# A row-wise infinity norm: implied waits dropped, a zeroing moved to GpSimd, a tail of 32 loads in place of 34

## Chip, cores, metric

One core of one Trainium2 chip. The metric is device time in microseconds (us) of one execution. The kernel before took 627.4 us (median of 3 runs, 627.34 to 628.16). A profile's span, from its first instruction to its last, is some 2.7 us shorter than the time; both are quoted as such.

## The reference

```python
rows, cols = 8192, 8192            # x is float32, 268.4 MB
np.linalg.norm(x, ord=np.inf, axis=1)   # per row: the largest absolute value
```

Every byte of x must be read once; the result is 32 KB.

## The kernel before

All loads are issued by SyncE (SP) into three buffers of 64 KB per partition, and VectorE (DVE) reduces them. 24 whole loads of 8.39 MB, the bulk, are reduced by one instruction each. The last 64 MiB, the tail, come in smaller and smaller loads, so that VectorE catches up with the stream: after the last byte only a small reduction should be left.

```python
TAIL = [
    [9728, 6656],
    [5632, 10752],
    [9600, 6784],
    [9344, 7040],
    [6784, 6528, 3072],
    [4736, 3072, 4224, 4352],
    [3968, 2432, 3072, 2944, 1792, 2176],
]
LAST = (
    [(0, w) for w in (2176, 2048, 1664, 1664)]
    + [(1, w) for w in (1536, 1280, 1152, 1024, 896, 896, 768)]
    + [(0, 640), (1, 640)]
)
...
    part = outp.tile([P, n_tail - B, k_max], F32)
    nc.vector.memset(part[:], 0.0)
...
    for a in range(A):                       # the bulk, 24 times in all
        for n in range(G):
            t = sbuf.tile([P, W + PAD], F32, tag="t")
            nc.sync.dma_start(out=t[:, :W], in_=x_b[a, n])
            absmax(r_bulk[:, a, n * B : (n + 1) * B], ...)
    for i, loads in enumerate(TAIL):         # partial maxima into part
        ...
            absmax(part[:, i * B + b, k : k + 1], t[:, lo : lo + n])
    for j, (b, w) in enumerate(LAST):        # the last buffer
        ...
        if j == len(LAST) - 4:               # store of the bulk maxima
            ins = nc.scalar.dma_start(out=out_b, in_=r_bulk[:])
            after(ins, done, mybir.DependencyClass.Sync)
    nc.sync.dma_start(out=out_t, in_=r_tail[:])
```

A load into a buffer that was used before waits for two things: that VectorE has read the buffer, and that the earlier load into it has landed. The second is implied by the first, since VectorE itself waited for that load. An instruction with two waits is issued as a separate EVENT_SEMAPHORE for one and the instruction itself with the other.

## Time and profile before

| | before |
|---|---|
| time, median of 3 | 627.4 us |
| span of the profile | 624.7 us |
| load queue, share of 16 DMA engines' time | 99.6% |
| VectorE busy | 89% |
| bulk: time between two landings (41 to 467 us) | 19.337 us, 433.8 GB/s |
| tail: last engine's landing of the 24th load to that of the last load | 156.27 us |
| SyncE's separate semaphore waits in the stream | 30, 17 ns each (one 28 ns) |

Two views carry the reading: the DMA row with its queue shares, which says that the stream never pauses, and the chain of waits in time order, where each "issue" of 0.02 us marks the landing that a reduction waited for. The prediction below shows these lines. In them DVE is VectorE, POOL is GpSimd, ACT is ScalarE, and SPq or DVEq is the sequencer that issues SyncE's or VectorE's instructions; q1 is the DMA queue of the loads, q10 that of the store of the bulk maxima and q14 that of the instruction fetches, each with its packets, MB and share of the 16 DMA engines' time. A load's landing is the moment at which its completion is reported.

### The profile page before, as it was taken

How to read it: one execution, taken by the hardware profiler on the slowest of the kernel's cores; microseconds unless marked ns; L12 is line 12 of the kernel's file. 1: busy time of each engine (PE TensorE's matmuls, PEld its weight loads, DVE VectorE, ACT ScalarE, POOL GpSimd, SP SyncE). 2: the span in 40 equal slices, each digit the busy share in tenths (PEclk: the TensorE clock that was granted, in tenths of full speed). 3: DMA queues.
4: the chain of work that ended last, by engine and by line, in shares of the span. 5: the costliest groups of instructions: out<-in, count | busy, mean ns of one | idle time of the engine just before them, and what ended most of it. 6: DMA issues, size and time to landing. Idle time of an engine off the chain costs nothing.

```text
span 624.7 us, 189 instructions
## 1 busy us (share of the span) xinstructions
DVE 553.0 (89%) x67; POOL 0.2 (0%) x4
## 2 busy tenths in 40 slices
DVE  0588988889988889888898888988889999999999
POOL 0000000000000000000000000000000000000000
DMA  9999999999999999999999999999999999999998
GB/s 403 462 411 453 420 449 424 432 441 403 470 403 470 403 470 403 453 420 453 420 441 432 424 449 403 470 403 470 403 438 425 445 417 443 421 427 432 423 423 342
DMA packets 9138, 268.48 MB, mean 430 GB/s; under 512 B 1712, under 2 KB 1712, under 8 KB 3248
## 3 DMA queue, kind: packets, MB, share of 16 engines
q1 hardware_dynamic: 8352, 268.44, 99.6%
q10 hardware_dynamic: 784, 0.02, 0.1%
q14 instruction: 2, 0.02, 0.0%
HBM read 268.44 MB, written 0.03 MB: 430 GB/s over the span
## 4 chain that ended last, share of the span: by engine, by line
DMA 67%; DVE 31%; issue 1%; another core or an unknown queue 0%; DVEq 0%; SPq 0%
DMA t<-in_x_dram 67%; DVE r_bulk L180 24%; DVE part L180 6%; DVE t L180 2%; DVEq L270 0%; DVE r_tail L180 0%; SPq L199 0%
## 5 line engine op out<-in xcount | busy, mean ns | idle before, releaser
L180 DVE TENSOR_REDUCE r_bulk<-t 128x2 f32<-128x16384 f32 x24 | 413.3, 17220 | 69.7 <-DMA t<-in_x_dram 69.7
L180 DVE TENSOR_REDUCE part<-t 128x1 f32<-128x8192 f32 (+20 forms) x28 | 121.5, 4411 | 0.3 <-DMA t<-in_x_dram 0.3
L180 DVE TENSOR_REDUCE t<-t 128x1 f32<-128x1664 f32 (+8 forms) x11 | 16.7, 1577 | 0.1
L180 DVE TENSOR_REDUCE r_tail<-t 128x1 f32<-128x644 f32 (+1 forms) x2 | 1.6, 818 | 0.0
L177 DVE MEMSET part<- 128x56 f32 x1 | 0.1, 105 | 0.9 <-PEq L259 0.9
L180 DVE TENSOR_REDUCE r_tail<-part 128x14 f32<-128x56 f32 x1 | 0.2, 202 | 0.0
L259 POOL MEMSET const-bfloat16-1.0<- 128x1 bf16 x1 | 0.1, 103 | 0.0
L259 POOL MEMSET const-uint8-127<- 128x1 uint8 x1 | 0.1, 102 | 0.0
L259 POOL MEMSET const-float32-0.0<- 128x1 f32 x1 | 0.1, 100 | 0.2 <-issue 0.2
L259 POOL MEMSET const-float32-1.0<- 128x1 f32 x1 | 0.1, 99 | 0.0
## 6 DMA issues: line engine op xcount, KB each, us to landing
t<-in_x_dram SPq DMA_DIRECT2D x2, 3392.0 KB, 37.2
t<-in_x_dram SPq DMA_DIRECT2D x1, 5376.0 KB, 40.5
t<-in_x_dram SPq DMA_DIRECT2D x1, 4864.0 KB, 32.9
t<-in_x_dram SPq DMA_DIRECT2D x1, 4800.0 KB, 32.8
t<-in_x_dram SPq DMA_DIRECT2D x1, 4672.0 KB, 34.7
t<-in_x_dram SPq DMA_DIRECT2D x3, 1536.0 KB, 36.9
t<-in_x_dram SPq DMA_DIRECT2D x1, 3520.0 KB, 42.7
t<-in_x_dram SPq DMA_DIRECT2D x1, 3328.0 KB, 40.4
```

The lines of the kernel that those rows point to most:

```text
L177: nc.vector.memset(part[:], 0.0)
L180: return nc.vector.reduce_max(out=o, in_=i, axis=X, apply_absolute_value=True)
L259: nc = _bacc.Bacc("TRN2", target_bir_lowering=False, num_devices=1)
```

## The change

Its intent: fewer instructions on SyncE and VectorE between a landing or a release and what follows it, no work for VectorE in the opening, and less overhead per transfer in the tail.

```diff
-    [9728, 6656],
-    [5632, 10752],
-    [9600, 6784],
+    [4736, 11648],
+    [12928, 3456],
+    [7040, 9344],
     [9344, 7040],
-    [6784, 6528, 3072],
-    [4736, 3072, 4224, 4352],
-    [3968, 2432, 3072, 2944, 1792, 2176],
+    [3584, 6784, 6016],
+    [5376, 4864, 1792, 4352],
+    [4096, 3584, 3200, 2944, 2560],
 ]
 LAST = (
-    [(0, w) for w in (2176, 2048, 1664, 1664)]
-    + [(1, w) for w in (1536, 1280, 1152, 1024, 896, 896, 768)]
-    + [(0, 640), (1, 640)]
+    [(0, w) for w in (2176, 1792, 1792, 1664)]
+    + [(1, w) for w in (1664, 1408, 1280, 1152, 1024, 896)]
+    + [(0, 768), (1, 768)]
 )
+def drop_implied_waits(nc):
+    ...                       # upto[n]: what VectorE had waited for by its n-th count
+            if i.engine == sp and own and len(waits) > 1:
+                known = upto[own - 1]
+                insts[n] = rewait(i, [s for s in waits
+                    if s.id == counter or s.wait_value > known.get(s.id, 0)])
+        elif i.engine == dve and own and len(waits) > 1:
+            ...               # a load that itself waited for VectorE's count implies it
+                insts[n] = rewait(i, [s for s in waits if s.id != counter])
+def clear_partials_early(nc):
+    ...                       # moves the memset ahead of GpSimd's drain, before the barrier
-    nc.vector.memset(part[:], 0.0)
+    nc.gpsimd.memset(part[:], 0.0)
+    nc.at_finalize(clear_partials_early)
+    nc.at_finalize(drop_implied_waits)
```

## The prediction

> **What bounds the kernel now.** I read the page first, for the busy shares and the DMA row; then the queue's share; then the chain of waits in order of time, for the two ends; then the waits of SyncE's queue and the views of single lines, for the waits that the change removes.
>
> ```profile
> span 624.7 us, 189 instructions
> DVE 553.0 (89%) x67; POOL 0.2 (0%) x4
> DMA  9999999999999999999999999999999999999998
> DMA packets 9138, 268.48 MB, mean 430 GB/s; under 512 B 1712, under 2 KB 1712, under 8 KB 3248
> q1 hardware_dynamic: 8352, 268.44, 99.6%
> q14 instruction: 2, 0.02, 0.0%
> ```
>
> VectorE is busy 89% of the span, the load queue 99.6% of sixteen engines' time, and no slice of the DMA row falls below 9 before the last. So the transfer of 268 MB is the bound, from the first packet to the last. A change that adds and removes no bytes can win only at the opening, after the last byte, or in what each transfer costs beyond its bytes. The next lines are from the chain of waits of the same kernel (start, length, what); an "issue" of 0.02 us ahead of a reduction is the landing of the load that it waited for.
>
> ```profile
> 41.24 0.02 issue
> ...
> 466.66 0.02 issue
> ...
> 612.24 0.02 issue
> 612.26 9.90 DVE t L180 x8
> 622.16 0.23 issue
> 622.39 0.59 DVE r_tail L180
> 622.98 0.08 issue
> 623.06 0.88 DVEq L270
> ```
>
> The second of the 24 whole loads landed at 41.24 us and the last at 466.66 us: 425.42 / 22 = 19.337 us for each 8.39 MB, 433.8 GB/s. The remaining 64 MiB is the tail, in 34 loads. Its last landing is the last of the four VectorE semaphore waits in this view of line L180, which ran at about 622.96 us:
>
> ```profile
> L180 DVEq EVENT_SEMAPHORE  x4: 21/21/21, 478.2 to 623.0; - x4
> L180 DVE TENSOR_REDUCE r_tail<-t x2: 817/818/820, 622.4 to 623.1; 128x1 f32<-128x644 f32 x1, 128x1 f32<-128x647 f32 x1
> ```
>
> So the tail took about 622.95 - 466.66 = 156.29 us where eight whole loads would take 8 x 19.337 = 154.70 us: 1.59 us more for 26 more loads, about 0.06 us each. Behind the last landing lie 0.17 us until the last reduction starts (623.12), its 0.82 us, and the output's transfer.
>
> **What the Trainium skill says.** "DMA: Bandwidth & Descriptors", section Specifications, gives the fabric ceiling into SBUF as 435 GB/s; the bulk loads at 433.8 GB/s sit at it, so the transfer rate has no room. (The same table's HBM limit per core, about 358 GB/s, does not agree: this trace reads faster.) "Perfetto Trace Analysis", section Sequencer-only Instruction, says that the profiler shows such an instruction's execution, not its wait; so the 17 ns of an EVENT_SEMAPHORE on SyncE is what is left of an extra wait once its semaphore is there. "VectorE: DVE Perf Modes", section on the TRN2 errata, gives VectorE reading SBUF a fixed cost of 58 cycles and one cycle an element at 0.96 GHz. Here the 768-element reduction starts at 621.53 and the next at 622.39: 0.86 us = 0.80 for the elements + 0.06, which agrees. "Runtime: NRT & Kernel Launch", section Instruction fetch mechanics, says that a sequencer fetches its further instructions by its own DMA queue, mostly hidden. The trace has such a queue with two packets (q14 above), each of 8 KB; by the packet records they ran at 592.0 and 609.4 us, in the midst of the tail.
>
> **The change part by part.**
>
> *Waits of SyncE.* The instruction order shows that all 21 later bulk loads lose the wait on the lane's previous landing and keep the one on VectorE, as do most first loads of the tail's buffers and the last store. Removed is mostly the separate EVENT_SEMAPHORE:
>
> ```profile
> L187 SPq EVENT_SEMAPHORE  x21: 17/17/17, 22.0 to 408.7; - x21
> DMA to landing us min/median/max: 22.0/40.7/59.4
> ```
>
> With lines 199, 224 and 242 there are 21 + 7 + 1 + 1 = 30 of them, of which I expect one to remain: 29 x 17 ns = 0.5 us of SyncE. None is on the path: they run as soon as the landing comes (the first at 22.0 us), and then SyncE waits up to 17.2 us for VectorE, which is the wait that stays:
>
> ```profile
> SPq L187 <- DVE r_bulk L180: 361.6, 21, 17.2
> SPq L187 <- DMA t<-in_x_dram: 54.8, 21, 20.1
> ```
>
> And a bulk load lands a median 40.7 us after its issue, twice its own 19.3 us, so it stands behind a whole load in the queue. Issuing it some 20 ns earlier moves no byte. Worth 0.
>
> *Waits of VectorE.* Two of its four separate waits go: on the first partial maximum and on the first load of the last buffer, each a few tens of ns, 123 and 17 us before the end. VectorE has caught up with the loads again by then or is behind for other reasons. The two waits ahead of the final reductions stay. Worth 0.
>
> *The memset.* 0.105 us leaves VectorE at 0.87 us, where VectorE waits until 22 us for data: 0. On GpSimd a memset of 42 elements comes ahead of the opening barrier. Its four others start 0.03 us apart, so this is 0.03 to 0.1 us, and SyncE's drain ends after GpSimd's anyway (0.43 + 0.126 = 0.56 against 0.30 + 0.18 = 0.48). Should it delay the barrier, it delays the second load's issue from 0.79 us, while the first load, issued at 0, keeps the queue busy to 22 us: 0.
>
> *The tail.* Two loads fewer, the same 64 MiB: 2 x 0.06 = 0.12 us earlier. The last two loads grow from 640 to 768 columns, so the last reduction grows from 647 to 774 elements, 127 x 1.04 = +0.13 us behind the last landing. I also ran the widths through an estimate built from the figures above (a landing every 0.06 us + 19.28 us per 16384 columns, a reduction start every 1.04 ns per element + 0.06 us): VectorE is no more than 0.03 us late at the last load of either list, and the ends differ by 0.01 us. The tail's recutting is thus a wash: -0.12 + 0.13.
>
> *Two side effects.* First, the instruction fetches. The 609.4 us one, by the landing records, set one DMA engine back some 0.9 us, which made it the last of the sixteen for all later loads by about 0.27 us. SyncE loses 31 of its 93 recorded instructions; if one of the fetches is SyncE's, it falls away or comes after the end. Whether that is the harmful one I cannot tell: at even odds, -0.13 us. Second, the store of the bulk maxima is released after the fourth load from the end. There are then 896 + 768 + 768 = 2432 columns to come instead of 768 + 640 + 640 = 2048, 0.45 us more of loading, so its 784 small packets may fall among the last loads where before they just missed them. They took 6 us together, 0.38 us on each engine; with turns taken packet by packet I put it at +0.05 to +0.3, say +0.1 us.
>
> Sum: 0 + 0 + 0 + (-0.12 + 0.13) - 0.13 + 0.1 = about -0.02 us. Leaning a little to the removed fetch, -0.1: 627.4 - 0.1 = 627.3 us.
>
> **The rivals.** (1) The dropped waits were binding and the loads now start early enough to matter: against it stands the DMA row of 9s and the queue's 99.6%. All idle engine time before the last landing, 0.4% or 2.5 us with both ends in it, would be the most to gain: 625 us. (2) VectorE becomes the bound of the tail, since it has larger pieces at the end and no spare wait: its busy row is 9 from slice 31 on, and 1.04 ns an element against 1.18 ns for a load leaves it 12% per element, less 0.06 us a piece. If it fell behind at the end by a piece, that would add up to 0.9 us: 628.3 us. (3) The store collides with the last loads in full and the fetch still hits: +0.4 us, 627.8 us. (4) The harmful fetch is gone and the store slips through: -0.3 us, 627.1 us.
>
> **Range and chances.** All mechanisms together span 626.8 to 628.0 us around 627.3. The three runs of before span 627.34 to 628.16, a scatter as large as any of these terms, upward. I take 626.6 to 628.1. Two per cent is 12.5 us, five times all the idle DMA time, so faster by that is all but excluded; slower needs a stall in the load queue that no part of the change brings, or a hidden cost in a run's state. Chances: 0.005, 0.985, 0.01.
>
> **What would show it right or wrong.** In the profile after: mean GB/s still 430 and the load queue at 99.6%; about 30 SyncE semaphore waits fewer with the median time from issue to landing of the bulk loads unchanged at 40.7 us (if it grew or the bulk loads landed closer than 19.34 us, rival 1 lives); VectorE's 69.7 us of waiting for bulk data unchanged; the last bulk landing at 466.6 us to within 0.1; the last landing near 622.8; the final reductions at about 0.95 us; the store's issue near 621.1. Fewer packets on the instruction queue would support the first side effect, an unchanged two with the same lag at the end would refute it. I would be wrong if the bulk landings move, or the end goes by more than 0.7 us with no step above to carry it.

## The result

| | before | changed |
|---|---|---|
| time, median of 6 runs | 627.62 us (627.34 to 628.16) | 627.43 us (627.33 to 628.26) |
| span of the profile | 624.7 us | 624.7 us |
| instructions in the profile | 189 | 154 |

The ratio is 0.9998, with a 95% interval from 0.9985 to 1.0011: the same. A ratio is the mean time of one kernel's fast runs over that of the other's of the same rounds, so not quite the ratio of the medians.

The page of the changed kernel, the same rows as in the prediction:

```profile
span 624.7 us, 154 instructions
DVE 552.6 (88%) x64; POOL 0.3 (0%) x5
DMA  9999999999999999999999999999999999999998
DMA packets 8849, 268.47 MB, mean 430 GB/s; under 512 B 1680, under 2 KB 1680, under 8 KB 3216
q1 hardware_dynamic: 8064, 268.44, 99.6%
q14 instruction: 1, 0.01, 0.0%
```

35 instructions are gone and the stream is the same: 99.6%, 430 GB/s, no slice below 9 before the last. The instruction queue has one packet in place of two. The changed kernel's chain of waits in time order (start, length, what):

```profile
41.29 0.02 issue
...
447.29 0.02 issue
...
621.92 0.20 issue
622.12 0.80 DVE r_tail L262
622.93 0.06 issue
622.99 0.94 DVE r_tail L262
```

The 2nd load lands at 41.29 us and the 23rd at 447.29: 406.00 / 21 = 19.333 us a load, against 19.337. The last reduction starts at 622.99 us, 0.13 us sooner than before (623.12), and takes longer, as the view of line L262 shows beside VectorE's separate waits, now two and not four:

```profile
L262 DVEq EVENT_SEMAPHORE  x2: 21/21/21, 621.9 to 622.9; - x2
L262 DVE TENSOR_REDUCE r_tail<-t x2: 943/944/945, 622.1 to 623.0; 128x1 f32<-128x772 f32 x1, 128x1 f32<-128x774 f32 x1
```

So it ends at 622.99 + 0.945 = 623.93 us, where before it ended at 623.12 + 0.820 = 623.94. And the waits of SyncE's queue (who for whom: us in total, times, longest):

```profile
SPq L269 <- DVE r_bulk L262: 417.2, 21, 37.5
```

Before, 361.6 us of this stood under VectorE and 54.8 us under the landings: 416.4 us, and now 417.2 us. SyncE waits as long as before, and now in one wait instead of two. The separate waits were gone, the waiting was not. Nor do the bulk's loads land sooner after their issue than before (22.0/40.7/59.4), as the view of the line that issues them shows:

```profile
DMA to landing us min/median/max: 22.0/40.7/59.5
```

The other signs named in the prediction came too: the 24th landing at 466.65 us, the last at 622.88, the store's issue at 621.24. VectorE's waiting for bulk data is 70.6 us and not 69.7, since without the memset its first wait counts from the start (22.0 us in place of 21.0).

### The profile page after: what moved, and what is told of

It is laid out like the page before. It is cut to its first block, busy times and chain, and to the rows that moved or that the text cites. A ratio compares the mean times of both kernels' runs of the same rounds, so it can differ in the third digit from the quotient of the medians.

```text
span 624.7 us, 154 instructions
## 1 busy us (share of the span) xinstructions
DVE 552.6 (88%) x64; POOL 0.3 (0%) x5
## 3 DMA queue, kind: packets, MB, share of 16 engines
q1 hardware_dynamic: 8064, 268.44, 99.6%
## 4 chain that ended last, share of the span: by engine, by line
DMA 64%; DVE 36%; issue 0%
DMA t<-in_x_dram 64%; DVE r_bulk L262 22%; DVE part L262 11%; DVE t L262 3%; DVE r_tail L262 0%
## 5 line engine op out<-in xcount | busy, mean ns | idle before, releaser
L262 DVE TENSOR_REDUCE r_bulk<-t 128x2 f32<-128x16384 f32 x24 | 413.3, 17220 | 70.6 <-DMA t<-in_x_dram 70.6
L262 DVE TENSOR_REDUCE part<-t 128x1 f32<-128x8192 f32 (+18 forms) x27 | 121.5, 4569 | 0.7 <-DMA t<-in_x_dram 0.7
L262 DVE TENSOR_REDUCE t<-t 128x1 f32<-128x1792 f32 (+7 forms) x10 | 16.2, 1687 | 0.0
L262 DVE TENSOR_REDUCE r_tail<-t 128x1 f32<-128x772 f32 (+1 forms) x2 | 1.8, 944 | 0.0
L262 DVE TENSOR_REDUCE r_tail<-part 128x14 f32<-128x42 f32 x1 | 0.2, 186 | 0.0
```

The lines of the kernel that those rows point to most:

```text
L262: return nc.vector.reduce_max(out=o, in_=i, axis=X, apply_absolute_value=True)
```

## The experiments

To compare parts of a tenth of a microsecond, the runs' times are too coarse, so I also read the landing records of each trace: every load has 16 landings, one from each DMA engine. "Tail" below is the mean of the 16 landings of the last load less the mean of the 24th load's; "lag" is how far the last engine's landing of the last load stands behind that mean; "end" is the time from that last landing to the end of the last reduction. A "fetch" is a packet on the instruction queue after the start.

| kernel | loads in tail | fetches, of which in tail | 24th landing, us | tail, us | lag, us | end, us |
|---|---|---|---|---|---|---|
| before | 34 | 2, 2 | 466.66 | 156.074 | 0.67 | 1.009 |
| before, repeated | 34 | 2, 2 | 466.71 | 156.067 | 0.45 | 1.019 |
| memset alone | 34 | 2, 2 | 466.86 | 156.067 | 0.75 | 1.017 |
| waits alone | 34 | 1, 1 | 467.00 | 156.035 | 1.19 | 0.965 |
| tail alone | 32 | 2, 2 | 467.30 | 155.974 | 0.71 | 1.072 |
| changed | 32 | 1, 1 | 466.65 | 155.928 | 0.78 | 1.053 |
| changed, repeated | 32 | 1, 1 | 466.82 | 155.926 | 0.81 | 1.053 |
| changed, 30 more VectorE instructions | 32 | 1, 0 | 467.12 | 155.876 | 0.80 | 1.051 |
| changed, store one load later | 32 | 1, 1 | 467.44 | 155.929 | 0.71 | 1.084 |

The tail's mean repeats to 0.01 us for the same number of loads and fetches; the 24th landing does not, and differs by 0.8 us over these rows without regard to the kernel.

### The waits alone

```diff
  # the kernel before, with the function as in the changed kernel
+    nc.at_finalize(drop_implied_waits)
```

> The kernel before with the implied waits dropped and nothing else. Main theory (the load stream is the bound and the dropped waits were already met when SyncE or VectorE came to them): time within 0.1% of before, bulk landings 19.34 us apart, SyncE's separate semaphore waits down from 30 to about 1. Of the two instruction fetches the one at 609 us is SyncE's, so this kernel shows one packet on the instruction queue and not two, the last engine no longer lags, and the last landing comes 0.2 to 0.3 us before 622.93 us. Rival (the waits were on the path): some 29 x 17 ns to 29 x 50 ns are won, 0.5 to 1.5 us, and the bulk landings move closer. Rival for the fetch (both fetches are VectorE's or neither depends on SyncE's count): two packets stay and the last landing stays at 622.9 us.

627.53 us against 627.42 us of before in the same rounds, ratio 1.0001 (0.9987 to 1.0015). The instruction queue's row of its page:

```profile
q14 instruction: 1, 0.01, 0.0%
```

And the waits of its SyncE queue, the row of the bulk's loads:

```profile
SPq L243 <- DVE r_bulk L236: 417.6, 21, 37.3
```

One separate wait is left on SyncE's loads, as foretold (the view of its loads' lines shows one EVENT_SEMAPHORE), and one fetch; SyncE waits 417.6 us for VectorE in the bulk and for nothing else there. The rival of waits on the path falls. The times alone could not exclude 0.5 us, but in the trace the bulk landings are 19.355 us apart and so not closer than the 19.337 before, and the tail is 0.04 us shorter. My forecast of the last landing was wrong, though: it came at 623.55 us, later than before's 622.93. By the means of 16 landings, +0.14 of these 0.62 us are the bulk (24th load), -0.04 the tail and +0.52 the lag, which rose from 0.67 to 1.19 us: the one fetch left hit an engine that stood 0.28 us behind the mean already and made it the last, at +1.21 us. So a removed fetch takes its time from the mean (156.035 against 156.07), but the last landing depends on which engine the other one hits.

### The memset alone

```diff
  # the kernel before
-    nc.vector.memset(part[:], 0.0)
+    nc.gpsimd.memset(part[:], 0.0)
+    nc.at_finalize(clear_partials_early)
```

> The kernel before with only the zeroing moved to GpSimd ahead of the barrier. Main theory: nothing but the opening changes; second load issued within 0.05 us of 0.79 us, first landing at 22.0 us, two instruction fetches, last landing at 622.9 us, span 624.7 us. Rival (the memset delays the barrier and with it the stream): second issue later by 0.1 us or more and every landing after the first later by as much.

One run, 627.66 us, beside a median of 627.42 us (627.32 to 627.71) for before on the same chip. The opening in the timeline (start, length, engine, line, operation):

```profile
0.00 1.14 SPq L223 DMA_DIRECT2D t<-in_x_dram  x2
0.37 0.14 POOL L213 MEMSET part<- 128x56 f32 x1
```

The memset takes 0.14 us at 0.37 us. The records have the second load's issue at 0.81 us, 0.02 us later than the 0.79 before, and the first landing at 21.99 us (21.96). Tail, fetches and end are those of before. The last landing and the span missed their forecasts by 0.3 us (623.22 and 625.0 us); 0.22 us of it stands in the mean of the 24th landing already, 0.07 us in the lag. The second landing is 0.04 us later than before's, not the 0.1 us or more of the rival. The part is worth nothing either way.

### The tail alone

```diff
  # the kernel before, with the changed TAIL and LAST
```

> The kernel before with only the new tail of 32 loads, all waits kept. Main theory: two loads fewer bring the last landing forward by 0.12 us, the later start of the last reduction's 0.945 instead of 0.820 us takes it back, time within 0.1% of before; two instruction fetches, the SyncE one again late in the tail. The store of the bulk maxima meets the last load and costs it about 0.05 us. Rival (the tail is where the change wins or loses, and another part cancels it): the span moves by more than 0.3 us either way.

627.58 us against 627.42, ratio 1.0004 (0.9991 to 1.0016). Its queue row keeps both fetches:

```profile
q14 instruction: 2, 0.02, 0.0%
```

The table gives the two terms cleanly. Two loads fewer are worth 156.07 - 155.974 = 0.10 us, 0.05 us each. The larger last piece costs 1.072 - 1.01 = 0.06 us. Both have the foretold sign; the second is half as large as I had it. The rival's sign came by its letter, for the profiled span is 625.4 us, 0.7 us more than before's. But 0.64 us of that is there at the 24th landing (467.30 us), before the new tail has an effect, and the last landing at 623.55 us is late for the same reason. So the rival, large parts that cancel, falls by the tail and the end in the table.

### Thirty more instructions on VectorE

```diff
  # the changed kernel; pad is a new [P, 1] tile, and clear_partials_early
  # is made to look at GpSimd's memsets alone
+    for _ in range(30):
+        nc.vector.memset(pad[:], 0.0)     # one column, in VectorE's idle opening
```

> The changed kernel with 30 one-column memsets on VectorE in the opening, in the 21 us in which it waits for the first load. Main theory (the remaining fetch is VectorE's, comes after a fixed number of its instructions, and sets one DMA engine back by the fetch plus about one packet of the load under way): the fetch moves from 587 us to about 290 to 320 us, into whole loads with packets of 2.42 us; one engine falls behind by 2.4 to 2.8 us for good; the last landing moves from 622.88 to about 624.8 us and the time to about 629.4 us (+0.3%). Rival 1 (the fetch is not VectorE's): it stays at 587 us and the time stays at 627.4 us. Rival 2 (it is VectorE's, but the cost does not depend on the packets): it moves and costs 0.9 us as before, time 627.4 us.

627.85 us against 627.42, ratio 1.0007 (0.9994 to 1.0019). The queues in the stretch from 290 to 300 us:

```profile
q1 hardware_dynamic: 81, 4.26, 98.7%
q14 instruction: 1, 0.01, 0.2%
```

The fetch moved from 586.95 us to 296.56 us. In both kernels 47 of VectorE's recorded instructions had started by then, while SyncE stood at 50 and at 19. So this fetch is VectorE's and comes at about the same count of its instructions (45 to 50 of the recorded ones over these traces). The other went with 29 of SyncE's instructions and two of VectorE's. It was no second one of VectorE's: before, it came 10 recorded VectorE instructions after the first, and here 53 more started after the fetch without another. It is then SyncE's by elimination.

The second half of my theory is refuted, rival 2 is right. The fetch ran 0.309 us, and the load packet behind it took 3.044 us instead of 2.418: 0.309 + 0.626 = 0.94 us for one engine. In the tail, with packets of 0.25 to 0.65 us, the same sum is 0.72 us and 0.92 us (before, the second with two slow packets behind the fetch), 0.98 us (changed) and 0.99 us (waits alone). A fetch sets one engine back by 0.7 to 1.0 us, whatever the packets. Over 16 engines that is about 0.05 us of the mean, which the table has: 155.928 with the fetch in the tail, 155.876 without.

### One buffer: the disputed waits on the path

```diff
  # the kernel before; for the second run also drop_implied_waits
-    BUFS: int = 3,
+    BUFS: int = 1,
```

> The kernel before with one load buffer instead of three, all waits kept: now every load waits for VectorE on the path that sets the time, so that a dropped wait has its best chance to show in the next run. A whole load should take 17.2 us of reduction + about 1 us until the first packet + 19.3 us, some 37.7 us instead of 19.34; in all about 1100 us.

> The same with one buffer and the implied waits dropped. Main theory (an implied wait is by its nature met before the wait that stays, so its 17 ns are over while SyncE still waits for VectorE): the bulk landings come as far apart as in the run with the waits kept, to within 0.02 us, and the time agrees within 0.1%. Rival (a dropped wait saves its own time even so, 17 to 60 ns in each of some 30 loads): 0.5 to 2 us less, landings 0.02 to 0.06 us closer.

1178.44 us with the waits kept, 1178.18 us with them dropped, ratios 1.8782 (1.8757 to 1.8808) and 1.8779 (1.8750 to 1.8808) to before's 627.40 us. The landings are 39.216 us apart with the waits and 39.223 us without: nothing gained in any load. The 0.26 us between the medians are less than the runs of either kernel differ among themselves (1178.35 to 1179.19 us and 1177.44 to 1179.41). The waits of SyncE's queue in the bulk, with the waits kept:

```profile
SPq L187 <- DMA t<-in_x_dram: 496.9, 23, 21.8
SPq L187 <- DVE r_bulk L180: 396.1, 23, 17.2
```

And with them dropped:

```profile
SPq L243 <- DVE r_bulk L236: 893.9, 23, 39.2
```

496.9 + 396.1 = 893.0 us in two waits, 893.9 us in one. While SyncE waits for the landing it would have to wait for VectorE anyway. The forecast of 37.7 us per load missed: I had counted 1 us until the first packet and the stream's 19.34 us. A load into an empty queue takes 22.0 us from issue to landing (39.22 - 17.22), like the very first one.

### Half the bulk's reductions

```diff
  # the changed kernel; the result is wrong on purpose
-                t[:, :W].rearrange("p (b c) -> p b c", b=B),
+                t[:, : W // 2].rearrange("p (b c) -> p b c", b=B),
```

> The changed kernel with bulk reductions over half of each tile; the result is wrong on purpose. VectorE's bulk work halves, 17.2 to 8.7 us a tile, and each buffer comes free 8.5 us earlier. Main theory (the load stream is the bound of the bulk): bulk landings 19.34 us apart as before, issue to landing 49 instead of 40.7 us, time 627.4 us within 0.1%. Rival (earlier issues are worth something, which is what dropping waits aims at): bulk landings closer, time below 626.5 us.

627.51 us against 627.40, ratio 1.0002 (0.9989 to 1.0014). From its groups by line (busy us, mean ns, idle before and its releaser):

```profile
L262 DVE TENSOR_REDUCE r_bulk<-t 128x2 f32<-128x8192 f32 x24 | 208.5, 8686 | 267.5 <-DMA t<-in_x_dram 267.5
```

And from the view of the line that issues the bulk's loads:

```profile
DMA to landing us min/median/max: 21.9/49.3/59.5
```

Buffers come free 8.5 us earlier, the loads are issued 8.5 us earlier, and they stand in the queue for the whole of it: 49.3 us from issue to landing, and landings 19.36 us apart. If 8.5 us at every issue are worth nothing, 17 ns are not worth more.

### Four microseconds more on VectorE in the tail

```diff
  # the changed kernel; pad is a new [P, 1] tile
+            if i == 0 and j == 0:
+                absmax(pad[:], t[:, :3780])
```

> The changed kernel with one extra reduction of 3780 columns, 4.0 us of VectorE, early in the tail. Theory that VectorE has little slack in the tail (an estimate by the recursion of the prediction: 0.97 us): the last reduction starts some 3.0 us later than the last landing needs, time about 630.4 us (+0.5%), last landing unchanged. Rival (the stream alone bounds the tail as it does the bulk): VectorE's lag is taken up by the end, time within 0.1%.

630.71 us against 627.40, ratio 1.0049 (1.0036 to 1.0061): 0.5% slower, with the last landing at 622.79 us (622.88 in the changed kernel). The end in the timeline:

```profile
624.14 0.41 ACTq L326 DMA_DIRECT2D out_dram<-r_bulk  x1
625.02 1.81 DVE L264 TENSOR_REDUCE r_tail<-t 128x1 f32<-128x772 f32 x2
626.86 0.35 SPq L328 DMA_DIRECT2D out_dram<-r_tail  x1
```

The output's transfer is issued at 626.86 us instead of 623.96, 2.90 us later. By the chain of waits the extra reduction holds VectorE for 4.00 us (its own record lasts 4.08, and the next one starts before its end), so 1.10 us were absorbed, beside my 0.97. The rival falls. The tail is a balance: the stream is its bound with about a microsecond to spare on VectorE.

### The store one load later

```diff
  # the changed kernel
-        if j == len(LAST) - 4:
+        if j == len(LAST) - 3:
```

> The changed kernel with the store of the bulk maxima released one load later, after the 896-column piece. Theory (in the changed kernel the store's packets fall among those of the last load and cost it about 0.05 us: that load landed 1.008 us after the one before it, the equally large one before it 0.960 us): the store issues at about 622.2 us, the last load lands 0.96 us after the one before it, nothing else moves. Rival (the spread between the last two landings is chance): still about 1.01 us.

One run, 628.18 us (its 24th landing was at 467.44 us, 0.8 us later than in the changed kernel, long before the edit can act). The store was issued at 623.1 us and not at 622.2, since all of this run came later. The last load landed 0.983 us after the one before it, where the changed kernel has 1.008 and 1.027 in its two traces. In the run with four more microseconds on VectorE, where the store came after all loads, it is 0.992 us. So the store costs the last load some 0.02 to 0.03 us; the other 0.02 to 0.03 us of the difference to 0.960 are the last load's own. The theory is half as large as I had it. Its picture of packets that collide is not what the records show: in the changed kernel only 3 load packets (4 in its repeat) ended after the store's first packet began, and every packet of the last two loads took 121 ns, with the store and without. By the means of 16 landings the last two loads are 0.990 and 0.993 us apart in the changed kernel and 0.988 and 0.987 us without the store among them, so the mean hardly moves. What comes later is the last engine's landing after its last load packet: 0.39 to 0.40 us in five traces with the store among the last landings (changed, changed repeated, tail alone, 30 more VectorE instructions, half reductions), 0.37 us in the two without. Why it comes later stays open.

### Both kernels once more

> The changed kernel once more, unchanged, for a second trace. If the scatter of some 0.7 us between profiles of different kernels lies in the bulk's load stream and not in the kernels, the landing of the 24th load moves by some tenths of a us against 466.65 us, while from there to the last landing it takes 156.2 us to within 0.1 us, with one instruction fetch, and from there to the end of the last reduction 1.05 us to within 0.03 us.

> The kernel before once more, unchanged. As for the repeat of the changed kernel: 24th landing anywhere from 466.6 to 467.3 us, two instruction fetches near 592 and 609 us, tail 156.3 us within 0.1 us, from the last landing to the end of the last reduction 1.01 us within 0.03 us.

The changed kernel took 627.40 us, before 627.14 us, one run each on the same chip, of unknown state. By the table their tails repeat to 0.007 us and 0.002 us, their ends to 0.01 us. Two expectations missed: I had put the tail up to the last landing at 156.3 us within 0.1 for before, and it came at 156.03, for the lag was 0.45 us and not 0.67. Both fetches were there at the same times, with the same extra packet times, and this time the later one hit an engine that stood further forward: the lag was 0.53 us right after that fetch, where in the first trace it was 0.74. The 24th landings scattered less than foretold here, 466.82 and 466.71 us.

No experiment points to a version that would beat both kernels by more than the scatter: the largest single term found is 0.1 us.

## Why the prediction was right

**The bound.** Right, and shown: with the bulk's buffers 8.5 us earlier nothing changes, and the page after has the same stream.

**The waits are worth 0.** Right, and shown three ways: the waits alone (1.0001), one buffer where every wait is on the path (39.216 against 39.223 us), and the unchanged sum of SyncE's waiting. VectorE's two waits were dropped together with SyncE's and not tested apart. Their times were misread in the prediction: they stand at 478.2 and 605.6 us, 146 and 19 us before the end of the span and not 123 and 17.

**The memset is worth 0.** Right by the trace of the part alone: 0.02 us on an issue that has 21 us to spare.

**The tail's recutting is a wash.** Right in its sum, off in its terms. Two loads fewer: forecast -0.12, measured -0.10 us. I had divided 1.59 us by 26, and part of the 1.59 us was the two fetches and their lag. The larger last reduction: forecast +0.13, measured +0.04 to +0.06 us. The reduction did grow by 0.125 us, but I had VectorE no more than 0.03 us late at the last load; before it started 0.19 us after the landing, in the changed kernel 0.11, so the new cut won back 0.08.

**The fetch.** The mechanism was right (one of the two is SyncE's and goes), and both terms of its size were off. The claim that the harmful one made an engine the last for good by about 0.27 us held for one trace; in its repeat the last engine ended only 0.04 us behind the next. What is sure is 0.04 to 0.05 us of the mean for each; the -0.13 us at even odds mixed this with the luck of which engine is hit (lag 0.45 to 1.19 us).

**The store.** Forecast +0.1, measured +0.02 to +0.03 us at the last landing, next to nothing in the mean, and without any load packet slowed.

Measured together: -0.14 us of the tail's mean (loads -0.10, fetch -0.04) and +0.04 us at the end, so -0.10 us beside a scatter of near 1 us between runs of one kernel. The lag is left out as luck. That the forecast leaned to -0.1 us as well is luck too: it leaned so for the fetch, which was sized about three times too large, as was the store with the opposite sign. The forecast 627.3 us and the measured 627.43 us agree within that scatter; that the kernel is 0.1 us faster is worked out from traces and not shown by times.

**The scatter.** I took it from the runs without a cause. The landing records place much of it in the bulk: the 24th landing moves between 466.65 and 467.44 us from trace to trace, also for kernels whose bulk is the same, with single load packets of 2.5 to 3.4 us in place of 2.42 (15 to 102 of 3072 in a trace). What the bulk's packets took beyond 2.418 us, shared over 16 engines, is 0.66 us in before and 1.56 us in the run with the later store; those 0.89 us match the 0.88 us by which the means of the 24th landing differ. What makes those packets slow stays open.

## What to carry to other kernels

A wait that is implied by another is met before it, so removing it saves no waiting; look at the sum of both waits before and after, and at whether the transfers behind it would have started earlier at all. Where the transfer queue is 99.6% busy, ask only what a change does to the bytes, to the number of transfers (0.05 us each here) and after the last landing. To judge tenths of a microsecond, compare means over the 16 engines between two landings in the trace; the last landing alone carries the luck of one engine, and the times the scatter of the whole stream.

## What the Trainium skill lacked or had wrong

- "Runtime: NRT & Kernel Launch", section Instruction fetch mechanics, calls a fetch mostly hidden and speaks of 16 KiB blocks. Here the fetches are single packets of 8 KB, and each sets one of the 16 DMA engines back by 0.72 to 0.99 us in a saturated stream, at about the same count of the engine's instructions (45 to 50 recorded ones of VectorE).
- "DMA: Bandwidth & Descriptors", section Specifications, has an HBM limit of about 358 GB/s per core without a condition; the bulk here, on one core, runs at 433.8 GB/s, at the fabric figure of the same table. The row is not wrong but lacks what the page's section Measured says, that about 358 GB/s is what each core gets when both cores of an HBM domain stream. The prediction's remark that it does not agree overlooked this.
- No page that I read gives the cost of one more load in a saturated stream: 0.05 us for loads of 128 rows here.
